# Hymba block on one core: the down projection's later groups add each product's bank straight onto the output tiles

## The chip, the core and the metric

The kernel runs on one core of a Trainium2 chip. The metric is device time in microseconds of one execution, as the median of several runs. A core has TensorE (PE in the profile; its weight loads are PEld), VectorE (DVE), ScalarE (ACT) and GpSimd (POOL), each with its own in-order queue, and SyncE (SP), whose queue issues this kernel's DMAs. TensorE writes its results to PSUM, which has eight banks of 128 x 512 float32 here; VectorE and ScalarE read them from there.

## What is computed

One decoder block on 2048 positions of width 1024, in float32: a normalised input projection, gated linear attention beside a short gated convolution, an output projection, and a SwiGLU feed-forward part. The change lies in the last product of the feed-forward part.

```python
def reference(x, norm1_g, w_in, ..., w_ffn_gate, w_ffn_up, w_ffn_down, norm_f_g):
    ...
        x = x + mixed
        h2 = rmsnorm(x, norm2_g[l])
        ffn = (jax.nn.silu(h2 @ w_ffn_gate[l]) * (h2 @ w_ffn_up[l])) @ w_ffn_down[l]
        x = x + ffn
    return rmsnorm(x, norm_f_g)
```

`w_ffn_down` is 2816 x 1024.

## The kernel before

All large products run with the positions as columns, 512 at a time, in two halves of two column blocks (j = 0, 1). Each float32 operand is split into a high and a low part (`split`, lines 152 to 154): ScalarE writes the high half (L153), VectorE the difference (L154). A product step (`product_step`) is then three matmuls: high by high, high by low, low by high (L381 to L383).

A `unit` computes a 2 x 2 block of outputs (two row tiles r, two column blocks j) with seven products in place of eight, by Strassen-Winograd combinations. `unit_weights` loads four raw quarters of the weights, lets GpSimd make four combinations (L364, L365, L366, L371), and splits seven operands into tiles `wq`, of which there are four buffers. Three PSUM banks serve a unit. Bank `oa` holds the first product and goes on being summed up through the third, fifth and seventh; bank `ob` takes the second and the sixth; the fourth has a bank of its own. In between, the banks are read: before the change, ScalarE copies (L401, in `copied`) take the first product as c11, the second as c22 and the sum of first and third as c12, into tiles of the pool `tp` or, with `into`, into tiles given by the caller. VectorE additions (L405, in `plus`) then add the fourth product to c11, bank `oa` as it stands after the fifth to c22, and bank `ob` after the sixth to c12. The fourth output, c21, is returned as the bank itself when there is no `into`. A product that goes on summing in a bank has to wait until that bank has been read.

The feed-forward part of a half is `ffn_up` (22 units over eleven column pairs m, whose results are split and stored in DRAM) and then `ffn_down`. The down projection's 2816 rows are cut into four groups of m: the first of two pairs, the three later ones of three (`GROUPS`). In each group four units run, one for each pair d0 of the eight row tiles of the output. The first group writes the output tiles y through `into`. The later groups call `unit` without it and add each result onto y (L982): c11, c22 and c12 by GpSimd, c21 by VectorE out of its bank; in the last group of the second half c12 goes to VectorE as well. In the second and third group GpSimd also adds the residual x1 onto two y tiles a unit (L989). In the last group of the first half every y is stored (`store`, L148), to be normalised later; in that of the second half ScalarE squares it (L790, L793), GpSimd sums the squares (L794), and the last four outputs are made by `last_unit`, which does not call `unit`. So 12 + 11 = 23 units belong to the later groups.

Seven of the eight y pairs of a half lie in slots of the pool `opp` (28 buffers), which also holds all operands; the next stage's operands (`load_h2`) are loaded into slots as they come free, on SP's queue behind the stores that were put ahead of them.

The code's order is not that of the engines: the framework plans the order of instructions on every engine ahead of time, from a simulated timeline (`schedule_with_timeline_sim=True`), and keeps data dependencies with semaphores. At run time each queue goes strictly in the planned order.

Of the kernel before, what the change touches and what calls it, by code (L numbers as in the profile page):

```python
# [14 lines left out]
ALU = mybir.AluOpType  # L15
# [36 lines left out]
def tile_hymba_block(ctx, tc, x, xt, win, wa, wgu, wout, wffn, wdown, wdown_first, small, out):  # L52
    nc = tc.nc
    act, dve, pool, pe = nc.scalar, nc.vector, nc.gpsimd, nc.tensor
# [80 lines left out]
    def bank(name="mm"):  # L135
        return ps.tile([P, PB], F32, name=name, tag="mm")

    def tt(name):
        return tp.tile([P, PB], F32, name=name, tag="t")

    def bt(name, shape=(P, PB)):
        return bx[0].tile(list(shape), F32, name=name, tag="b")

    def load(dst, src):
        return nc.sync.dma_start(dst, src)

    def store(dst, src):
        return nc.sync.dma_start(dst, src)  # L148
# [67 lines left out]
    def tick():  # L216
        pace[0] += 1
        if pace[0] % 2 == 0 or hurry:
            step()
        elif ahead and pace[0] % 4 == 1:  # L220
            next(ahead[0], None)
# [9 lines left out]
    def drain_background(until=lambda: False):  # L231
        while background and not until():
            step()
# [124 lines left out]
    def unit_weights(src):  # L358
        raw = raw_weights(src)
        n = src.shape[-1]  # L360
        a11, a12, a22, a21 = [raw[:, i, :] for i in range(4)]
        s1 = rawp.tile([P, PB], F32, name="s1", tag="s1", bufs=1)[:, 0:n]
        w = {"A11": weight_quarter(a11)}
        pool.tensor_tensor(s1, a21, a22, ALU.add)  # L364
        pool.tensor_tensor(a21, a11, a21, ALU.subtract)  # L365
        pool.tensor_tensor(a11, s1, a11, ALU.subtract)  # L366
        w["S1"] = weight_quarter(s1)
        w["S2"] = weight_quarter(a11)
        w["A12"] = weight_quarter(a12)
        w["S3"] = weight_quarter(a21)  # L370
        pool.tensor_tensor(a12, a12, a11, ALU.subtract)  # L371
        w["S4"] = weight_quarter(a12)
        w["A22"] = weight_quarter(a22)
        return w

    def product_step(o, w, op, k, first):
        n = len(op)
        c = slice(k * P, (k + 1) * P)
        wh, wl = w[:, 0, c], w[:, 1, c]
        xh, xl = op[k][:, 0, :], op[k][:, 1, :]  # L380
        pe.matmul(o[:], wh, xh, start=first and k == 0, stop=False, skip_group_check=True)  # L381
        pe.matmul(o[:], wh, xl, start=False, stop=False, skip_group_check=True)  # L382
        return pe.matmul(o[:], wl, xh, start=False, stop=k == n - 1, skip_group_check=True)  # L383

    def unit(src, ops, into=None):


        w = unit_weights(src)

        def mul(i, o=None):  # L390
            first = o is None
            o = bank() if first else o
            n, m = PRODUCTS[i]
            for k in range(len(ops[m])):
                product_step(o, w[n], ops[m], k, first)
            tick()
            return o

        def copied(name, o, at):
            t = tt(name) if into is None else into[at]  # L400
            act.activation(t[:], o[:], AF.Copy)  # L401
            return t

        def plus(t, o):
            dve.tensor_tensor(t[:], o[:], t[:], ALU.add)  # L405
            return t


        oa = mul(0)
        c11 = copied("c11", oa, (0, 0))  # L410
        ob = mul(1)
        c22 = copied("c22", ob, (1, 1))
        mul(2, oa)
        c12 = copied("c12", oa, (0, 1))
        plus(c11, mul(3))
        mul(4, oa)
        plus(c22, oa)
        mul(5, ob)
        plus(c12, ob)
        mul(6, oa)  # L420
        if into is not None:
            copied("c21", oa, (1, 0))
        return [(0, 0, c11, False), (1, 1, c22, False), (0, 1, c12, False), (1, 0, oa, True)]

# [101 lines left out]
    def build_h():  # L526


        def quad(k, j):
            return scaled(col(C_G1 + k), rbs[j], raws[j, k])  # L530

        return build_first(quad, first_weights)
# [255 lines left out]
    def sum_squares(ssq, y, first):  # L788
        if first:
            act.activation(ssq[:], y, AF.Square)  # L790
        else:
            q = tt("q")
            act.activation(q[:], y, AF.Square)  # L793
            pool.tensor_tensor(ssq[:], ssq[:], q[:], ALU.add)  # L794
# [138 lines left out]
    def act_op(half, m, n):  # L933
        o = opp.tile([P, 2, PB], F32R, name="op", tag="op")
        load(o[:].bitcast(F32), s_act[half][m][n][:])
        return o

    def ffn_down(half):

        y, early = {}, {}  # L940

        def group_op(m, n):
            return early.pop((m, n)) if (m, n) in early else act_op(half, m, n)

        for u, m0 in enumerate(GROUPS):
            ms = range(m0, m0 + (3 if u else 2))
            last = m0 == LAST_GROUP
            if last:
                drain_background()
            ops = {n: [group_op(m, n) for m in ms] for _, n in PRODUCTS}  # L950
            if last and half:
                begun = set()
                ssq = [
                    tiny.tile([P, PB], F32, name=f"ssx{j}", tag=f"ssx{j}", bufs=1) for j in range(2)
                ]
            for d0 in range(0, KD, 2):
                src = wdown[4 * u - 4 + d0 // 2] if u else wdown_first[d0 // 2]
                if u == 0 and d0 == 2:

                    order = [(m, n) for _, n in PRODUCTS for m in range(GROUPS[1], GROUPS[2])]  # L960
                    for m, n in order[:EARLY]:
                        early[m, n] = act_op(half, m, n)
                if u == 0:
                    for d in (d0, d0 + 1):
                        if d < KD - 1:
                            pair = opp.tile([P, 2, PB], F32, name="y", tag="op")
                        for j in range(2):
                            y[d, j] = pair[:, j, :] if d < KD - 1 else bt("y")[:]
                    unit(src, ops, {(r, j): y[d0 + r, j] for r in range(2) for j in range(2)})
                    continue  # L970
                xs = []
                if u < 3:
                    for d in (d0, d0 + 1):
                        xs.append((y[d, u - 1], bt("x1")))
                        load(xs[-1][1][:], s_x1[2 * half + u - 1][d][:])
                if last and half and d0 == KD - 2:
                    last_unit(src, ops, [act_op(half, m, "B12") for m in ms], y, ssq)
                    break
                for r, j, c, p in unit(src, ops):
                    yy = y[d0 + r, j]  # L980
                    eng = dve if p or last and half and r != j else pool
                    eng.tensor_tensor(yy, c[:], yy, ALU.add)  # L982
                    if last and half:
                        sum_squares(ssq[j], yy, j not in begun)
                        begun.add(j)
                    elif last:
                        store(s_x1[2 * half + j][d0 + r][:], yy)
                for yy, x1 in xs:
                    pool.tensor_tensor(yy, x1[:], yy, ALU.add)  # L989
        if half == 0:  # L990
            ahead[:] = [finish_later(half)]

    def finish_later(half):

        ssq = [
            tiny.tile([P, PB], F32, name=f"ssx{j}", tag=f"ssx{j}", bufs=1) for j in range(2)
        ]
        for j in range(2):
            for d in range(KD):
                y = bt("y")  # L1000
                load(y[:], s_x1[2 * half + j][d][:])
                yield
                sum_squares(ssq[j], y[:], d == 0)
        yield
        rb = [bank("rb_ps"), None]
        yield from both_rstd(ssq, rb)
        for j in range(2):
            if j:
                rb[1] = bank("rb_ps")
                act.activation(rb[1][:], ssq[1][:], AF.Copy)  # L1010
            for d in range(KD):
                y = bt("y")
                load(y[:], s_x1[2 * half + j][d][:])
                yield
                dve.scalar_tensor_tensor(y[:], y[:], col(C_GF + d), rb[j][:], ALU.mult, ALU.mult)
                store(out[2 * half + j, :, d, :], y[:])
# [59 lines left out]
    ops, first, differences = build_h()  # L1076
# [9 lines left out]
    ops = load_pairs(s_h1)  # L1086
# [122 lines left out]
```

## Time and profile before

| | us |
|---|---|
| median of 3 runs | 2098.65 |
| lowest and highest run | 2098.31, 2102.15 |
| profiled execution, its own time | 2102.39 |
| its span, first to last instruction | 2100.5 |
| TensorE busy in the span | 2034.6 |
| later groups of the first half, about | 1257 to 1435 of the span |
| later groups of the second half, about | 1900 to 2067 of the span |

Rows of groups read: line, engine, operation, output<-inputs, shapes, count | busy us, mean ns of one | idle time of the engine before them, and what ended it. Rows of waits read: who <- for whom: us in total, times, longest. Rows of a timeline read: start, duration, engine, line, operation, tiles, [idle time before <- what ended it]. A matmul's row of 0.39 us overlaps with the next; the distance of starts is what a matmul takes. DVE, ACT and POOL rows of L153 and L154 are the weight splits; tiles named c are results of a unit, y the output tiles, wq split weights, raw weights as loaded, mm a bank. Lines are those of the kernel before.

### The profile page before, as it was taken

What the parts mean: (1) busy time and instruction counts of PE and PEld (TensorE: products, weight loads), DVE (VectorE), ACT (ScalarE), POOL (GpSimd) and SP (SyncE); (2) the same over time, 40 slices, a digit from 0 to 9 for tenths busy, and PEclk for the clock granted to TensorE, in tenths of its full rate; (3) what the DMA queues carried; (4) which work ended last, traced back from release to release, by engine and by line L of the source; (5) the groups of instructions that cost most, each with busy time, mean ns of one, the idle gap of its engine ahead of it and who ended that gap; (6) DMA issues with size and microseconds to landing.
All of it is one profiled execution on the core that took longest, in us unless ns stands there. A gap on an engine that the chain in (4) does not pass through costs nothing.

```text
span 2100.5 us, 26873 instructions
## 1 busy us (share of the span) xinstructions
PE 2034.6 (97%) x9133; PEld 1649.8 (79%) x9133; DVE 1420.2 (68%) x1983; ACT 1003.2 (48%) x1990; POOL 971.9 (46%) x703
## 2 busy tenths in 40 slices
PE   6999999999999999999999999999999999999996
PEld 4768888877888878788888878787888888877774
DVE  7669786549743786788887665555767766665554
ACT  6555455656542345545545443333545444453344
POOL 3436322222102464465464338774655445436764
PEclk9999999999999999999999999999999999999998
DMA  7359495425686873655646687698444554587673
GB/s 279 129 167 318 128 340 158 149 81 167 205 281 236 325 251 105 236 200 214 223 175 220 236 314 269 234 344 321 159 178 165 192 210 174 213 340 271 259 270 110
DMA packets 189241, 464.43 MB, mean 221 GB/s; under 512 B 19824, under 2 KB 65072, under 8 KB 179504
## 3 DMA queue, kind: packets, MB, share of 16 engines
q1 hardware_dynamic: 189104, 462.72, 61.1%
q8 instruction: 72, 1.18, 0.2%
q14 instruction: 65, 0.53, 0.1%
HBM read 297.49 MB, written 165.15 MB: 220 GB/s over the span
## 4 chain that ended last, share of the span: by engine, by line
PE 74%; DVE 10%; DMA 8%; issue 3%; POOL 3%; ACT 3%; SPq 0%; DVEq 0%; POOLq 0%; ACTq 0%
PE mm L381 22%; PE mm L383 22%; PE mm L382 22%; DVE wq L154 2%; DVE h L508 2%; PE mm L812 1%; DVE op L154 1%; PE mm L813 1%; PE mm L815 1%; DVE so L154 1%; DMA raw<-in_wffn_dram 1%; DMA raw<-in_wdown_dram 1%; DMA op<-shT 1%; PE a_ps L576 1%; DVE c L405 1%
## 5 line engine op out<-in xcount | busy, mean ns | idle before, releaser
L381 PE MATMUL mm<-op,wq 128*128 128x512 f32 x2499 | 981.6, 395 | 17.8 <-ACT wq L153 7.4
L382 PE MATMUL mm<-op,wq 128*128 128x512 f32 x2499 | 976.9, 391 | 0.0
L383 PE MATMUL mm<-op,wq 128*128 128x512 f32 x2499 | 966.4, 392 | 10.4 <-DVE wq L154 9.6
L154 DVE TENSOR_TENSOR wq<-raw,wq 128x512 fp32r<-128x512 f32 (+2 forms) x626 | 527.7, 850 | 333.2 <-ACT wq L153 330.4
L153 ACT ACTIVATE wq<-raw 128x512 fp32r<-128x512 f32 (+2 forms) x626 | 363.5, 587 | 548.6 <-PE mm L383 391.5
L381 PEld LDWEIGHTS mm<-op,wq 128*128 128x128 f32 x2499 | 471.1, 189 | 132.0 <-ACT wq L153 13.5
L383 PEld LDWEIGHTS mm<-op,wq 128*128 128x128 f32 x2499 | 471.1, 189 | 121.2 <-DVE wq L154 22.6
L382 PEld LDWEIGHTS mm<-op,wq 128*128 128x128 f32 x2499 | 471.1, 189 | 97.0 <-issue 1.0
L366 POOL TENSOR_TENSOR raw<-s,raw 128x512 f32<-128x512 f32 (+2 forms) x97 | 127.6, 1316 | 422.6 <-DVE wq L154 402.5
L405 DVE TENSOR_TENSOR c<-mm,c 128x512 f32<-128x512 f32 x267 | 183.0, 685 | 94.4 <-PE mm L383 92.1
L364 POOL TENSOR_TENSOR s<-raw 128x512 f32<-128x512 f32 (+2 forms) x97 | 129.4, 1334 | 205.3 <-DMA raw<-in_wffn_dram 98.7
L371 POOL TENSOR_TENSOR raw<-raw 128x512 f32<-128x512 f32 (+2 forms) x97 | 126.8, 1307 | 129.6 <-DVE wq L154 122.4
L401 ACT ACTIVATE c<-mm 128x512 f32<-128x512 f32 x267 | 155.0, 586 | 39.0 <-PE mm L383 37.7
L794 POOL TENSOR_TENSOR ssx<-ssx,q 128x512 f32<-128x512 f32 x52 | 75.8, 1470 | 158.7 <-ACT q L793 158.5
L365 POOL TENSOR_TENSOR raw<-raw 128x512 f32<-128x512 f32 (+2 forms) x97 | 135.1, 1392 | 4.0
L982 POOL TENSOR_TENSOR y<-c,y 128x512 f32<-128x512 f32 x66 | 98.7, 1497 | 57.3 <-DVE c L405 53.2
L154 DVE TENSOR_TENSOR so<-t,so 128x512 fp32r<-128x512 f32 x100 | 90.7, 913 | 24.4 <-ACT so L153 24.0
L153 ACT ACTIVATE wq<-s 128x512 fp32r<-128x512 f32 (+2 forms) x97 | 56.8, 586 | 98.7 <-PE mm L383 86.0
L812 PE MATMUL mm<-op,wq 128*128 128x512 f32 x256 | 100.9, 395 | 0.0
L813 PE MATMUL mm<-op,wq 128*128 128x512 f32 x256 | 99.8, 390 | 0.0
L154 DVE TENSOR_TENSOR wq<-s,wq 128x512 fp32r<-128x512 f32 (+2 forms) x97 | 84.0, 866 | 17.0 <-ACT wq L153 16.4
L153 ACT ACTIVATE so<-t 128x512 fp32r<-128x512 f32 x100 | 62.5, 626 | 37.8 <-DMA sa_B<-so 16.1
(181 smaller groups left out, 1880.3 us busy)
## 6 DMA issues: line engine op xcount, KB each, us to landing
raw<-in_wffn_dram SPq DMA_DIRECT2D x44, 1024.0 KB, 6.1
sa_T<-so SPq DMA_DIRECT2D x88, 512.0 KB, 4.9
op<-sa_T SPq DMA_DIRECT2D x88, 512.0 KB, 9.4
sa_B<-so SPq DMA_DIRECT2D x69, 512.0 KB, 3.4
op<-sa_B SPq DMA_DIRECT2D x69, 512.0 KB, 9.0
raw<-in_win_dram SPq DMA_DIRECT2D x23, 1024.0 KB, 5.4
raw<-in_wdown_dram SPq DMA_DIRECT2D x24, 768.0 KB, 6.1
sx<-y SPq DMA_DIRECT2D x48, 256.0 KB, 3.3
```

What stands on the lines that cost most here:

```text
L153: last_hi[:] = [act.activation(hi, src, AF.Copy)]
L154: return dve.tensor_tensor(lo, src, hi.bitcast(F32), ALU.subtract)
L364: pool.tensor_tensor(s1, a21, a22, ALU.add)
L365: pool.tensor_tensor(a21, a11, a21, ALU.subtract)
L366: pool.tensor_tensor(a11, s1, a11, ALU.subtract)
L371: pool.tensor_tensor(a12, a12, a11, ALU.subtract)
L381: pe.matmul(o[:], wh, xh, start=first and k == 0, stop=False, skip_group_check=True)
L382: pe.matmul(o[:], wh, xl, start=False, stop=False, skip_group_check=True)
L383: return pe.matmul(o[:], wl, xh, start=False, stop=k == n - 1, skip_group_check=True)
L401: act.activation(t[:], o[:], AF.Copy)
L405: dve.tensor_tensor(t[:], o[:], t[:], ALU.add)
L812: pe.matmul(o[e, j][:], wh, m[:, 0, :], start=k == 0, stop=False)
```

## The change

`unit` gets a second way to deliver: with `onto`, a dictionary of output tiles, `copied` does not copy but adds the bank onto the tile with VectorE, and the three later `plus` calls add onto the same tiles, since `copied` returns them. With `onto`, as with `into`, the fourth result is taken out of its bank by `copied` as well. The later groups pass their y tiles as `onto`; the loop that followed keeps the sums of squares and the stores, and loses its additions. Each of the 23 units has then seven VectorE additions from PSUM onto y, and no L401 copy and no GpSimd addition of its results. Inputs, products and DMAs are the same; the order in which the summands reach y is another.

```diff
-    def unit(src, ops, into=None):
+    def unit(src, ops, into=None, onto=None):
...
         def copied(name, o, at):
+            if onto is not None:
+                return plus(onto[at], o)
             t = tt(name) if into is None else into[at]
             act.activation(t[:], o[:], AF.Copy)
             return t
...
         plus(c12, ob)
         mul(6, oa)
-        if into is not None:
+        if into or onto:
             copied("c21", oa, (1, 0))
         return [(0, 0, c11, False), (1, 1, c22, False), (0, 1, c12, False), (1, 0, oa, True)]
...
-                for r, j, c, p in unit(src, ops):
+                onto = {(r, j): y[d0 + r, j] for r in range(2) for j in range(2)}
+                for r, j, *_ in unit(src, ops, onto=onto):
                     yy = y[d0 + r, j]
-                    eng = dve if p or last and half and r != j else pool
-                    eng.tensor_tensor(yy, c[:], yy, ALU.add)
                     if last and half:
                         sum_squares(ssq[j], yy, j not in begun)
                         begun.add(j)
```

## The prediction

> **What bounds the kernel now.** I read the page's busy table first, then the busy time by stretches of the span, then the waits of TensorE, then the timeline around the longest of them.
>
> ```profile
> span 2100.5 us, 26873 instructions
> PE 2034.6 (97%) x9133; PEld 1649.8 (79%) x9133; DVE 1420.2 (68%) x1983; ACT 1003.2 (48%) x1990; POOL 971.9 (46%) x703
> ```
>
> TensorE is busy 97% of the span, and the change leaves its matmuls as they are. So the change can only move the time in which TensorE stands still or runs at a reduced clock. The stretches say where that is; columns are engine busy time, granted clock, DMA share and rate.
>
> ```profile
> core 0: us, PE busy (x) PEld busy (x) DVE busy (x) ACT busy (x) POOL busy (x), PEclk, DMA share, GB/s
> 1000.00:1195.00 195.00, 194.78 (x859) 160.86 (x858) 146.19 (x174) 97.45 (x172) 99.66 (x68) 1.00 0.54 200
> 1257.00:1435.00 178.00, 176.99 (x776) 144.74 (x775) 97.43 (x134) 62.87 (x124) 131.25 (x101) 1.00 0.79 297
> 1435.00:1480.00 45.00, 41.76 (x174) 33.18 (x173) 24.53 (x26) 17.55 (x32) 23.98 (x17) 0.96 0.56 217
> 1480.00:1880.00 400.00, 397.58 (x1744) 326.57 (x1744) 279.39 (x360) 196.42 (x354) 194.40 (x139) 1.00 0.57 207
> 1900.00:2067.00 167.00, 161.55 (x695) 130.12 (x694) 93.57 (x123) 66.55 (x130) 121.14 (x95) 0.99 0.63 237
> ```
>
> The second and fifth rows (1257 to 1435 and 1900 to 2067) hold the later groups of the two down projections, 23 units in all: the only place that the change edits. TensorE stands idle there for 178.00 - 176.99 = 1.0 us and 167.00 - 161.55 = 5.5 us. The first and fourth rows are stretches of the gate/up projection, used below as a yardstick. GpSimd is at 74% and 73% in the two edited stretches, against 51% and 49% in the yardsticks; VectorE at 55% and 56% against 75% and 70%.
>
> Who TensorE waits for in 1900 to 2067, and the longest of these waits in TensorE's timeline, with what ScalarE and GpSimd did shortly before:
>
> ```profile
> PE mm L381 <- ACT c L401: 2.9, 2, 2.6
> ...
> PE mm L381 <- ACT wq L153: 2.3, 2, 1.8
> ```
>
> ```profile
> 1924.80 1.29 POOL L982 TENSOR_TENSOR y<-c,y 128x512 f32<-128x512 f32 x1
> ...
> 1928.59 0.99 POOL L366 TENSOR_TENSOR raw<-s,raw 128x384 f32<-128x384 f32 x1
> ...
> 1929.61 1.35 ACT L153 ACTIVATE wq<-raw 128x384 fp32r<-128x384 f32 x3 [0.55 <-POOL raw L366]
> ...
> 1930.18 0.50 PE L381 MATMUL mm<-op,wq 128*128 128x512 f32 x1 [1.76 <-ACT wq L153]
> ...
> 2034.41 0.39 PE L383 MATMUL mm<-op,wq 128*128 128x512 f32 x1
> 2037.38 0.62 PE L381 MATMUL mm<-op,wq 128*128 128x512 f32 x1 [2.59 <-ACT c L401]
> ...
> 2036.21 0.63 ACT L793 ACTIVATE q<-y 128x512 f32<-128x512 f32 x1 [0.83 <-DVE y L982]
> 2036.75 1.07 ACT L401 ACTIVATE c<-mm 128x512 f32<-128x512 f32 x2
> ```
>
> The clock just after 2037, as a row of the same view by stretches:
>
> ```profile
> 2037.60:2041.00 3.40, 3.40 (x9) 2.61 (x9) 0.45 (x1) 0.83 (x2) 2.80 (x3) 0.50 0.74 231
> ```
>
> At 2037 a bank's copy (L401) stood in ScalarE's queue behind a square (L793) that itself waited for an output tile; after that wait the clock is at 0.50 for 3.40 us, which costs another 3.40 x 0.50 = 1.7 us. At 1930 split weights were late: ScalarE waited for GpSimd's combination L366, which had stood behind output additions (L982). So the loss in the edited stretches is 1.0 + 5.5 + 1.7 = 8.2 us. That is the ceiling of what the edit can give inside them.
>
> **The change, part by part.** The groups of the two stretches, first half then second half:
>
> ```profile
> L405 DVE TENSOR_TENSOR c<-mm,c 128x512 f32<-128x512 f32 x36 | 24.8, 688 | 17.0 <-PE mm L383 17.0
> ...
> L982 DVE TENSOR_TENSOR y<-mm,y 128x512 f32<-128x512 f32 x12 | 8.2, 686 | 6.1 <-PE mm L383 6.0
> ...
> L982 POOL TENSOR_TENSOR y<-c,y 128x512 f32<-128x512 f32 x36 | 55.0, 1531 | 30.4 <-DVE c L405 30.3
> ...
> L401 ACT ACTIVATE c<-mm 128x512 f32<-128x512 f32 x37 | 21.6, 583 | 12.0 <-PE mm L383 12.0
> ...
> L982 POOL TENSOR_TENSOR y<-c,y 128x512 f32<-128x512 f32 x30 | 43.7, 1457 | 26.9 <-DVE c L405 22.9 <-DMA raw<-in_wdown_dram 2.2 <-DMA x<-sx 1.8
> ...
> L982 DVE TENSOR_TENSOR y<-c,y 128x512 f32<-128x512 f32 x3 | 2.0, 679 | 0.0
> ```
>
> *Removed:* 23 x 3 = 69 ScalarE copies at 0.583 us (40 us), 66 GpSimd additions (55.0 + 43.7 = 98.7 us) and three VectorE additions in the last group. All of it lies beside TensorE's work, so only the 8.2 us can come back. *Added:* 69 VectorE additions from a bank, at the 0.688 us of L405, so 69 - 3 = 66 more VectorE instructions, 45 us net. They lie beside the products too: a unit is 7 products of 9 matmuls, and at 195.00 us for 859 matmuls (0.227 us each) a product lasts 2.04 us. VectorE's load becomes (97.4 + 36 x 0.688) / 178 = 69% and (93.6 + 30 x 0.688) / 167 = 68%, still below the 75% and 70% at which the yardstick stretches lose only 0.22 and 2.42 us of TensorE. Were that cover gone, the 66 additions would cost their 45 us.
>
> It may be less load than that. The weight splits on VectorE differ widely from one to the next:
>
> ```profile
> L154 DVE TENSOR_TENSOR wq<-raw,wq x74: 542/583/1664, 1257.2 to 1434.8; 128x384 fp32r<-128x384 f32 x68, 128x512 fp32r<-128x512 f32 x6
> ...
> L405 DVE TENSOR_TENSOR c<-mm,c x267: 659/685/693, 83.5 to 2060.7; 128x512 f32<-128x512 f32 x134
> ...
> 1259.12 1.02 POOL L365 TENSOR_TENSOR raw<-raw 128x384 f32<-128x384 f32 x1
> ...
> 1259.20 1.35 DVE L154 TENSOR_TENSOR wq<-raw,wq 128x384 fp32r<-128x384 f32 x1 [1.45 <-ACT wq L153]
> ```
>
> A split reads two SBUF tiles and takes 0.54 to 1.66 us (1.35 in the last row, beside a GpSimd addition); an addition that reads a bank takes 0.66 to 0.69 wherever it stands. The change removes 98.7 of GpSimd's 131.3 + 121.1 us, so fewer splits should meet it. I book nothing for it.
>
> *Added wait.* Three times a unit a later product reuses a bank that ScalarE's copy used to free (the third, fifth and sixth product); now VectorE's addition frees it. Behind such an addition stand, in VectorE's queue, the low halves of the next unit's weights (L154), for which TensorE waits in turn. The existing code has one such release in a unit (the seventh product behind `plus(c22, oa)`), and the waits for L405 over the whole kernel are:
>
> ```profile
>   PE mm L381: 2.2, 3
> ```
>
> That is 2.2 us over (267 + 24) / 3 = 97 units, 0.023 us each; for 69 releases 1.6 us. The bounds: 0 if the 2.04 us of the product between hides all, and 69 x (0.688 - 0.583) = 7.2 us if the longer release lay open every time. I take 1.6, the rate of the same operation in this kernel. [...]
>
> *Moved.* The y tiles of the first half's last group are final without GpSimd, so 12 of their 16 stores on SP's queue can go earlier, past the loads of the next stage's operands behind them. TensorE's waits in 1435 to 1480:
>
> ```profile
> PE mm L381 <- ACT c L401: 1.7, 1, 1.7
> PE mm L381 <- DMA op<-shT: 1.5, 1, 1.5
> ...
> 1457.40:1460.70 3.30, 3.30 (x8) 2.61 (x9) 2.57 (x4) 1.44 (x3) 1.27 (x1) 0.50 0.64 206
> ```
>
> The stretch loses 45.00 - 41.76 = 3.2 us and 3.30 x 0.50 = 1.7 us of clock: 4.9. Bounds 0 and -4.9. I take 0: most operand loads wait for slots that only TensorE's last products free, and the DMA engines are 79% busy up to 1435. No DMA is added. The ScalarE squares and GpSimd's sums of squares keep their number; what is late next where GpSimd falls away is the weight chain of ScalarE and VectorE.
>
> *The sum.* After the change I expect the edited stretches to lose what the yardsticks lose, (0.22 + 2.42) / 595 x 345 = 1.5 us, and 1.6 us for the new releases: 3.1 in place of 8.2, a gain of 5.1 us. The profiled execution took 2102.39 us (span 2100.5 and 1.9 around it), so it would take 2097.3; it is 3.7 above the median of 2098.65, and I carry the gain over to the median: **2093.6 us**.
>
> **The rivals.**
>
> *Earlier stores as well.* The transition's 4.9 us fall away too: 2088.7. For it: a wait for an operand's landing there. Against: the busy DMA engines.
>
> *The loss stays, or isn't in the median run.* The profiled execution is 3.7 us over the median; if its long stall and slow clock at 2037 make that difference, only 5.1 - 3.7 = 1.4 us remain: 2097.3. The same holds if the new instruction order, which is planned afresh, brings back weights that come late, since 2.3 us of TensorE's waits are for them.
>
> *The slow clock isn't the wait's.* The rows show TensorE idle for 2.59 us and then the clock at 0.50. If the slow stretch comes anyway, 1.7 us of the gain go: 2095.3. [...] Both slow stretches quoted follow an idle TensorE, so the trace rather speaks against that.
>
> *Slower: VectorE's queue is the bound.* If an addition that frees a bank stands behind two drawn-out splits, it ends 2 x 1.66 + 0.69 = 4.0 us after its product, 2.0 us beyond the product between, and TensorE stops for that. Without new waits the gain is 8.2 - 1.5 = 6.7 us, so 4 such events eat it, and from 6 it is slower by more than 0.2%. At one in three units, 8 x 2.0 = 16, it is 9.3 us slower: 2108. For it: VectorE takes all seven releases and is strictly in order. Against: the yardsticks, where it is busier and releases one bank a unit.
>
> **How the numbers follow.** Chances: forecast 0.38, earlier stores 0.08, loss stays 0.25, clock 0.06, slower 0.23. A measurement of this kernel can tell about 0.2%, 4.2 us. The forecast lies just beyond that at 2094.45, and I count a little of it as no change: faster 0.44, same 0.33, slower 0.23. The range goes from 2087, a little below the second case, to 2106, which takes in the slower case up to 7 events and leaves its tail out. The forecast's own range is 2091 to 2096, from releases that cost nothing to 4 us.
>
> **What would show it.** No L401 and no GpSimd row with y<-c,y between 1257 and 1435 or 1900 and 2067; about 36 and 30 more L405 there, at 0.69 us; GpSimd's share falling from 74% to about 43% (131.3 - 55.0 of 178); TensorE idle in both together under 3 us, with no clock of 0.50 around 2037. A wait of PE for L405 of more than 5 us in these stretches would show the slower case, a wait for weights of the old size the third. The prediction is wrong if the stalls move to a place that no row here shows, such as the last 34 us.

## The result, and the profile after

| | before | after |
|---|---|---|
| median of 6 runs, us | 2101.72 | 2090.53 |
| lowest and highest, us | 2098.31, 2104.18 | 2085.95, 2092.94 |
| profiled execution, its own time, us | 2102.39 | 2092.78 |
| ratio to before, 95% interval | | 0.9935 (0.9923 to 0.9947) |

By the ratio the change makes the kernel faster by 0.65%, that is 13.7 us of 2101.72, with 11.1 to 16.2 as the interval's ends; the two medians differ by 11.2. The page of the changed kernel begins:

```profile
span 2090.8 us, 26872 instructions
PE 2029.0 (97%) x9133; PEld 1648.4 (79%) x9133; DVE 1434.0 (69%) x2049; ACT 970.1 (46%) x1921; POOL 876.7 (42%) x637
```

VectorE has 66 instructions more, ScalarE 69 and GpSimd 66 fewer, as the diff says. Line numbers after the edit are larger by two in the edited part of `unit` and up to the edited loop, where L405 is now L407 and L401 is L403, and by one behind it. The kernels of the experiments have line numbers of their own. Busy time by stretches, placed by the same work as in the prediction's table (the stretch 1195 to 1257 of before, the first group of the first half, is added, as 1198.8 to 1259.3):

```profile
core 0: us, PE busy (x) PEld busy (x) DVE busy (x) ACT busy (x) POOL busy (x), PEclk, DMA share, GB/s
...
1198.80:1259.30 60.50, 58.09 (x251) 46.37 (x250) 39.99 (x64) 29.19 (x64) 21.21 (x22) 1.00 0.87 339
1259.30:1435.70 176.40, 176.10 (x775) 144.99 (x774) 105.29 (x168) 46.94 (x90) 78.17 (x65) 1.00 0.79 301
1435.70:1478.50 42.80, 40.63 (x174) 31.81 (x173) 23.70 (x26) 17.52 (x32) 23.35 (x16) 1.00 0.57 223
1478.50:1878.40 399.90, 397.48 (x1745) 326.60 (x1744) 278.69 (x360) 195.95 (x354) 195.37 (x139) 1.00 0.57 207
1898.30:2057.50 159.20, 158.48 (x696) 129.95 (x695) 100.01 (x151) 52.53 (x99) 79.34 (x65) 1.00 0.65 250
```

The two edited stretches hold 1471 matmuls in both kernels and went from 178.0 + 167.0 = 345.0 us to 176.4 + 159.2 = 335.6: 9.4 us. The transition behind the first went from 45.0 to 42.8, the first group's stretch from 62.0 to 60.5. GpSimd is busy for 44% and 50% of the edited stretches. TensorE's waits in the first and the second of them are now these alone:

```profile
PE mm L383 <- DVE wq L154: 0.3, 1, 0.3
...
PE mm L383 <- DVE wq L154: 0.6, 1, 0.6
```

None is for a bank's release. The groups of VectorE in the first edited stretch, after:

```profile
L407 DVE TENSOR_TENSOR y<-mm,y 128x512 f32<-128x512 f32 x82 | 56.5, 690 | 62.8 <-PE mm L383 62.7
L154 DVE TENSOR_TENSOR wq<-raw,wq 128x384 fp32r<-128x384 f32 x68 | 44.2, 649 | 5.7 <-ACT wq L153 5.7
```

and one row of before that the prediction did not show:

```profile
L154 DVE TENSOR_TENSOR wq<-raw,wq 128x384 fp32r<-128x384 f32 x68 | 54.1, 804 | 49.7 <-ACT wq L153 49.7
```

The same 68 weight splits take 649 ns each in place of 804, 10 us less on VectorE; in the second half's later groups the mean falls from 859 to 707. The additions from a bank stay at 0.69 us. GpSimd's additions are gone there, but that is not the whole of it: with these additions moved to VectorE and the copies left alone (`e1_adds_only` below), the first half's splits still take 734 ns:

```profile
L154 DVE TENSOR_TENSOR wq<-raw,wq 128x384 fp32r<-128x384 f32 x67 | 49.0, 734 | 34.8 <-ACT wq L153 34.6
```

VectorE's idle time now lies in front of the additions, 62.7 us of waiting for TensorE's products, and hardly in front of the splits, 5.7 us of waiting for high halves in place of 49.7. That this means weights made ahead of need is not shown by the row alone: it falls to 12.6 with the copies on VectorE too (`e2_copies_only`), where no time is gained.

Runs of most kernels here spread over 6 to 11 us, so I compare stretches of the traces, one execution each, beside the times. The table gives the time between the same two matmuls, counted in the order of their starts (the 5401st, 5621st, 6401st, 6601st, 8391st and 9061st, and the end of the span), as worked out from the starts in each trace; under "before" in us, the others as a difference from it. "After, once more" is `e0_after`; the rows below it are the runs of the next section.

```
                    first    later     transition  gate/up   later     end
                    group    groups    behind it   second    groups
                    half 1   half 1                half      half 2
before              55.4     180.0     50.7        411.3     161.8     36.8
after               -1.6      -1.5     -2.2         -0.2      -8.1      0.0
after, once more     0.0      -1.4     -1.7         +1.6      -8.6      0.0
additions only      -1.6      -1.0     +0.1         +1.8      -1.1     +0.4
copies only          0.0      +0.7     +1.6         -0.4      +0.4     -0.6
first half only     -1.6      -1.3     -0.2         -0.1      +0.8      0.0
second half only    -1.6      +0.1     +0.2         +2.2      -8.9      0.0
squares later        0.0       0.0     +0.1         -0.1      -3.6      0.0
additions, squares  -1.6      -1.3     -2.1         +2.5      -5.6     +0.5
releases later      -1.5      +2.4     -1.3         +0.2      +1.8     +0.1
additions doubled   -1.6     +53.5     -3.4         +0.1     +47.9     +1.9
end reordered       -1.6      -1.2     -2.0         +2.0      -8.7     -4.1
```

The changed kernel's row adds up to -13.6 us, but its span is only 9.7 us shorter: this execution reached the first of these matmuls 3.8 us later (1208.5 against 1204.7). No edit touches the code up to there, and the twelve executions differ in it by 7 us (1201.3 to 1208.5), so part of the spread of times has nothing to do with the edits. The columns of the later groups hang on the edit; with the transition they make 11.8 us in one execution of the changed kernel and 11.7 in the other. The first and the fourth column jump by 1.5 to 2.5 whatever the edit is. In the first column, before and the second execution of the changed kernel have a stretch of half clock there (PEclk 0.50) and the first execution of the changed kernel has not (1.00), which is taken up in the last section; that the fourth jumps for the same reason is my estimate, from the 1.7 us (3.4 x 0.50) that such a stretch costs.

### The profile page after: what moved, and what is told of

It reads as the page before. It is cut to its first block, busy times and chain, and to the rows that moved or that the text cites. A ratio compares the mean times of both kernels' runs of the same rounds, so it can differ in the third digit from the quotient of the medians.

```text
span 2090.8 us, 26872 instructions
## 1 busy us (share of the span) xinstructions
PE 2029.0 (97%) x9133; PEld 1648.4 (79%) x9133; DVE 1434.0 (69%) x2049; ACT 970.1 (46%) x1921; POOL 876.7 (42%) x637
## 4 chain that ended last, share of the span: by engine, by line
PE 77%; DVE 10%; DMA 6%; issue 3%; ACT 2%; POOL 2%; SPq 1%; DVEq 0%; ACTq 0%; POOLq 0%
PE mm L381 22%; PE mm L383 22%; PE mm L382 22%; DVE wq L154 2%; DVE h L510 2%; PE mm L814 2%; PE mm L815 2%; PE mm L817 2%; DMA op<-shT 1%; DVE so L154 1%; DVE op L154 1%; PE a_ps L578 1%; DMA shT<-so 1%; SPq L145 1%; PE o_ps L738 1%
## 5 line engine op out<-in xcount | busy, mean ns | idle before, releaser
L383 PE MATMUL mm<-op,wq 128*128 128x512 f32 x2499 | 962.4, 391 | 11.7 <-DVE wq L154 11.2
L154 DVE TENSOR_TENSOR wq<-raw,wq 128x512 fp32r<-128x512 f32 (+2 forms) x626 | 506.7, 815 | 243.2 <-ACT wq L153 241.4
L407 DVE TENSOR_TENSOR y<-mm,y 128x512 f32<-128x512 f32 x185 | 127.4, 689 | 123.3 <-PE mm L383 122.6
L407 DVE TENSOR_TENSOR c<-mm,c 128x512 f32<-128x512 f32 x198 | 135.6, 685 | 64.6 <-PE mm L383 63.3
L796 POOL TENSOR_TENSOR ssx<-ssx,q 128x512 f32<-128x512 f32 x52 | 76.2, 1479 | 160.7 <-ACT q L795 160.5
L403 ACT ACTIVATE c<-mm 128x512 f32<-128x512 f32 x198 | 114.8, 586 | 16.2 <-PE mm L383 14.8
L154 DVE TENSOR_TENSOR wq<-s,wq 128x512 fp32r<-128x512 f32 (+2 forms) x97 | 79.7, 822 | 4.1 <-ACT wq L153 3.5
```

The source lines that it names most:

```text
L154: return dve.tensor_tensor(lo, src, hi.bitcast(F32), ALU.subtract)
```

## The experiments

**One part at a time.** First, GpSimd's additions go to VectorE and ScalarE's copies stay (`e1_adds_only`, on the kernel before):

```diff
-                    eng = dve if p or last and half and r != j else pool
+                    eng = dve
```

> The kernel before with one part of the change: the additions of c11, c22 and c12 onto y go from GpSimd to VectorE (two SBUF inputs); ScalarE's copies stay. Theory 1, two separate queues: GpSimd's additions held up the weight combinations, ScalarE's copies stood behind squares. Then this part takes away the waits for late weights at 1343 (1.2 us) and 1930 (2.0) and some of the transition (up to 2.7), and leaves the wait for L401 near 2037 with its slow clock (4.5): 3 to 6 us faster than before. Theory 2, the bank release by ScalarE was all: 0 to 1 us faster. Theory 3, a new plan of the order moves stalls at random: any sign, with stalls at new places.

Measured: ratio 0.9989 (0.9978 to 1.0001), 2.3 us faster with the interval touching zero, below the 3 to 6 of theory 1, though the interval reaches 4.6; in the later groups 1.0 and 1.1 us. Second, the copies go to VectorE and GpSimd's additions stay (`e2_copies_only`):

```diff
...
         def copied(name, o, at):
             t = tt(name) if into is None else into[at]
-            act.activation(t[:], o[:], AF.Copy)
+            if later:
+                dve.tensor_copy(t[:], o[:])
+            else:
+                act.activation(t[:], o[:], AF.Copy)
...
-                for r, j, c, p in unit(src, ops):
+                for r, j, c, p in unit(src, ops, later=True):
```

> The kernel before with the other part: in the later groups the three copies of a unit go from ScalarE to VectorE, GpSimd's additions stay. Theory 1: the wait for L401 near 2037 and its slow clock fall away (4.5 us, with the one at 2053 5.1), the late weights stay: 4 to 6 us faster than before, GpSimd still at about 73% in the later groups. Theory 2: nearly the whole gain, 9 to 13 us faster. Theory 3: any sign.

Measured: ratio 0.9997 (0.9987 to 1.0007), no change; +0.7 and +0.4 us in the later groups. Neither part alone comes near 13.7 us. Theory 2 falls, and so does theory 1's sum of two separate gains, whose 4 to 6 us for the copies did not come. Theory 3 can't be ruled out for a single run, since each edit has the order planned anew; against it, the first and the fourth column of the table differ from before by less than 1 us once 1.7 us are set aside for a half clock. The waits of TensorE in the second half's later groups with the additions on VectorE, and then with the copies on VectorE, its longest waits with each:

```profile
PE mm L381 <- ACT c L401: 3.3, 2, 2.2
PE mm L383 <- DVE wq L154: 1.6, 2, 0.9
```

```profile
PE mm L381 <- DVE c L402: 3.0, 2, 2.7
PE mm L381 <- ACT wq L153: 2.8, 3, 1.7
```

The wait for late weights shrinks where GpSimd is relieved, as theory 1 said. But the wait for the bank's copy stays in both, behind ScalarE's copy in the one and behind VectorE's in the other. So the copy was not the cause; it only stood last in a chain. That chain, from the trace with the copies on VectorE, in order of time (start, duration, what; here L793 and L796 are squares, L985 the additions onto y, L408 the addition from a bank into c and L402 the copy):

```profile
2028.16 1.54 POOL y L985
...
2029.73 0.02 ACT ssx L793
...
2030.27 0.52 ACT wq L153
...
2030.81 0.56 DVE wq L154
2031.37 0.60 DVE c L408
2031.97 0.97 DVE wq L154
2032.94 0.61 DVE y L985
...
2033.57 0.64 ACT q L796
...
2034.87 0.52 ACT wq L153
...
2035.41 0.57 DVE wq L154
2035.98 0.60 DVE y L985
2036.58 0.67 DVE wq L154
2037.25 0.61 DVE c L402
...
2037.90 0.50 PE mm L381
```

It goes in a circle through in-order queues. A square on ScalarE waits for an output tile y; behind the square stand high halves of weights; VectorE's low halves wait for those; and behind a low half stands the addition that makes the next y. The two laps here, from one y to the next, last 4.8 us (2028.16 to 2032.94) and 3.0 us, and at the end TensorE stops. In the kernel before, the chain ahead of the stop at 2037 makes the same laps, from GpSimd's addition at 2027.75 over the squares at 2033.17 and 2036.21, and ends in ScalarE's copy.

**One half at a time**, on the changed kernel, with the old loop where `onto` is None (`e3_first_half`, and `e4_second_half` with `half == 1`):

```diff
+                onto = onto if half == 0 else None
...
```

> The change in the first half's down projection alone. By the two traces of before and after, TensorE gained there 1.0 us in the later groups and 2.7 in the transition behind them: 3 to 4 us faster than before if these are the change's own; within 1 us of before if they are chance, above all the slow clock at 1457.

> The change in the second half's down projection alone. By the two traces TensorE gained 7.9 us there: 7 to 9 us faster than before if the stalls at 1930 and 2037 stand in every execution; 3 to 5 if the stall at 2037 and its slow clock come only in some. With the first half alone it should add up to the whole change, about 11 to 13 us.

Measured: 0.9969 (0.9956 to 0.9981) for the first half, 0.9955 (0.9941 to 0.9968) for the second: 6.5 and 9.5 us, together 16.0, within the whole change's interval but above the 11 to 13 expected; the first half alone was expected at 3 to 4. In the traces the first half's later groups give 1.3 us and the transition 0.2, the second half's groups 8.9. The rest of the first half's 6.5 us I can't lay to the edit: its profiled execution was already 3.4 us ahead of before's when it reached the first group. In the second half alone TensorE hardly stands still at all:

```profile
1902.00:2063.00 161.00, 160.91 (x707) 132.17 (x706) 99.36 (x152) 54.88 (x101) 79.49 (x65) 1.00 0.65 248
```

**The squares behind the next weights.** To test the circle, the kernel before with the squares of a unit put behind the next unit's splits in ScalarE's queue (`e8_squares_later`); copies and additions are those of before:

```diff
...
-                for r, j, c, p in unit(src, ops):
+                us = unit(src, ops)
+                if last and half:
+                    with tc.issue_after(last_hi[0].ins):
+                        for yy, j in waiting:
+                            sum_squares(ssq[j], yy, j not in begun)
+                            begun.add(j)
+                    waiting = []
+                for r, j, c, p in us:
...
                     if last and half:
-                        sum_squares(ssq[j], yy, j not in begun)
-                        begun.add(j)
+                        waiting.append((yy, j))
```

> The kernel before with one edit: in the second half's last group the squares of a unit's outputs stand in ScalarE's queue behind the next unit's weight splits. Copies, VectorE additions and GpSimd additions are those of before. The first four runs left open what the stall at 2037 is, since it stays at 2.6 us with the additions on VectorE and at 3.1 with the copies on VectorE. Theory A: a square that waits for an output tile holds the high halves of the weights behind it, and the output tile comes late because it takes copy, addition and addition after its product. Then moving the squares takes the stall at 2037 and its slow clock away (4.5 us, and 0.5 at 2053): 3 to 6 us faster than before. Theory B: the order or the load of VectorE alone does it, the squares don't matter: within 1 us of before, the stall at 2037 stays over 2 us.

The same edit on top of the additions by VectorE (`e9_both`):

> The additions of c11, c22 and c12 onto y by VectorE in place of GpSimd, and the squares behind the next unit's splits; ScalarE's copies stay. By theory A this joins the two reliefs, late weights behind GpSimd's additions and squares at the head of ScalarE's queue, and comes near the whole change: 7 to 12 us faster than before. By theory B it is like the additions alone: 0 to 5 us faster.

Measured: 0.9996 (0.9985 to 1.0007) for the squares, so the time alone shows no gain; 0.9976 (0.9964 to 0.9987), 5.0 us, for both, below the expected 7 to 12. The traces say more. With the squares moved, TensorE's waits in the second half's later groups are

```profile
PE mm L381 <- ACT wq L153: 2.2, 2, 1.8
PE mm L383 <- DVE wq L154: 1.5, 1, 1.5
```

The waits for L401 are gone, with ScalarE's copies still in place, and so is the half clock (PEclk 1.00 there). In return five squares now stand at one spot ahead of a high half, and TensorE waits for the low half that is made from it:

```profile
2058.65 0.50 PE L383 MATMUL mm<-op,wq 128*128 128x512 f32 x1 [1.45 <-DVE wq L154]
```

The stretch gains 3.6 us in this execution. With GpSimd relieved as well it gains 5.6, near the 1.1 + 3.6 = 4.7 of the two parts, as two separate hold-ups would give. Theory A holds for the place: the square is what led to the stop at 2037 and its half clock. It does not hold for the times: the interval leaves the squares alone at most 3.2 us of the expected 3 to 6. The remaining 2.5 to 3.3 us up to the whole change's 8.1 to 8.9 take in the new wait behind the moved squares, which with both edits is the longest of

```profile
PE mm L383 <- DVE wq L154: 2.5, 3, 1.5
```

Whether the copies have a share of their own was not tried.

**The price of an addition that frees a bank.** On the changed kernel, VectorE makes one more addition of the same bank, into a tile that nobody uses, ahead of the first, second and third addition of a unit (`e5_late_release`), and then ahead of all seven (`e6_all_doubled`, the same line inside `plus`):

```diff
             if onto is not None:
+                if name != "c21":
+                    dve.tensor_tensor(tt("junk")[:], o[:], onto[at], ALU.add)
                 return plus(onto[at], o)
```

> The changed kernel with one suspected cost raised: ahead of the additions that free a bank for a later product (first, second and third product of a unit) VectorE makes one more addition of the same bank into a tile that nobody uses, 69 in all at 0.69 us. The results are the same. If the 2.04 us of the product between hide the release with room to spare, as the changed kernel's trace without a wait for these additions says: within 3 us of the changed kernel (about 2091). If VectorE's queue is close to being the bound: 69 x 0.3 to 0.7, 20 to 48 us slower than the changed kernel.

> The changed kernel with all seven additions of a unit in the later groups doubled in the same way, 161 more at 0.69 us, 111 us of VectorE. Its load in the later groups rises from 60% to over 90%, and a product's share, two additions and a split, 2 x 0.69 + 0.65 = 2.03 us, comes to the 2.04 us that a product lasts. If the price of an addition decides only from there: 5 to 30 us slower than the changed kernel. If it is hidden even then: within 3 us. If VectorE was the bound already: the whole 111 us.

Measured: 1.0007 (0.9995 to 1.0019), so these 69 additions, 48 us of VectorE, take back the whole gain; against the changed kernel's 0.9944 in its second timing that is about 13 us, between the two expectations, on average 0.19 us for each. The trace has the loss in a few places. TensorE's waits for these additions in the second half's later groups are

```profile
PE mm L381 <- DVE y L409: 6.1, 4, 3.7
```

and two of them, 3.75 us at 2039 and 1.48 us at 2057, make most of it, with a half clock behind the first (starts 0.43 us apart from 2041.25 on). In the first half such waits are 0.8 us, and the 2.4 us of the table are mainly a stop for late weights at the very end of its column.

With all doubled, 1.0487 (1.047 to 1.0504), 102 us slower than before and some 114 slower than the changed kernel. The expectations of a hidden price fail. The size is that of the third case, in which VectorE is the bound and the whole 111 us show, but VectorE is not full. The later groups of the first half with the releases late, and with all additions doubled:

```profile
1259.00:1437.00 178.00, 175.93 (x772) 144.15 (x771) 125.50 (x201) 46.84 (x89) 77.36 (x64) 1.00 0.80 299
```

```profile
1259.00:1487.00 228.00, 188.31 (x759) 150.34 (x758) 161.16 (x249) 46.08 (x87) 73.75 (x64) 0.93 0.64 237
```

VectorE is busy for 71% in both, in the second because the stretch has grown with the stops; within the changed kernel's 176.4 us the same work would be 91%, so it would still fit. With all doubled, VectorE's timeline shows the additions in bunches, here three unused ones and then three onto y, and the chain has TensorE starting again only behind the second of those:

```profile
1345.76 1.89 DVE L408 TENSOR_TENSOR junk<-mm,y 128x512 f32<-128x512 f32 x3
1347.56 0.55 DVE L154 TENSOR_TENSOR wq<-raw,wq 128x384 fp32r<-128x384 f32 x1
1348.02 1.88 DVE L409 TENSOR_TENSOR y<-mm,y 128x512 f32<-128x512 f32 x3
```

```profile
1349.36 0.50 PE mm L381
```

TensorE's waits for them in the first and the second half's later groups are

```profile
PE mm L381 <- DVE y L409: 38.5, 11, 3.6
...
PE mm L381 <- DVE y L409: 37.1, 11, 4.1
```

about one a unit, 75.6 us in all. Half clock follows these waits (PEclk 0.93 over the 228 us of the first stretch, 0.91 over 230 in the second), which costs another 16 + 21 = 37 us. Waits and half clock make up the loss. With the releases late there were two such bunches ahead of a stop. That the bunching decides, and not the higher load as such, is my reading of the traces; a higher load in another order was not tried.

**The end of the kernel.** The profile of the changed kernel, like that of before, shows six scalings of the first column block on VectorE ahead of the last product's addition (L1060). The end with one edit, the scalings behind that addition (`e7_tail`), next to the changed kernel itself in the same session (`e0_after`):

```diff
-                dve.tensor_tensor(yy, o[:], yy, ALU.add)
+                added = dve.tensor_tensor(yy, o[:], yy, ALU.add)
...
         for j in range(2):
-            scale(j, rbs[j])
+            with tc.issue_after(added.ins):
+                scale(j, rbs[j])
```

> The changed kernel with one more edit at its end: the scaling of the first column block by VectorE stands behind the last product's addition. In the profile of the changed kernel, as in that of before, six scalings (3.7 us) stand ahead of that addition while TensorE has long finished, and the end of the kernel hangs on it. Expected: 3 to 4 us faster than the changed kernel if the six scalings then fit into the waits of the last normalisation; 0 to 1 if they are only moved to the end.

> The changed kernel once more, as the reference for the others on the same chip: 11 to 16 us faster than before.

Measured: `e0_after` 0.9944 (0.9927 to 0.9962), 2090.18 us median, 11.8 us faster than before; `e7_tail` 0.9926 (0.9913 to 0.9938), 2085.88 us, and the end shorter by 4.1 us in the trace, near the expected 3 to 4. VectorE's timeline at the end of the changed kernel, then with the edit:

```profile
2071.03 3.68 DVE L1043 TENSOR_TENSOR y<-y,rb 128x512 f32<-128x512 f32 x6 [0.66 <-ACT ssx L1037]
2074.63 0.68 DVE L1060 TENSOR_TENSOR y<-mm,y 128x512 f32<-128x512 f32 x1
2078.86 0.69 DVE L201 TENSOR_SCALAR ssx<-tot 128x512 f32<-128x512 f32 x1 [3.55 <-ACT l L199]
```

```profile
2068.67 0.69 DVE L1060 TENSOR_TENSOR y<-mm,y 128x512 f32<-128x512 f32 x1 [0.30 <-PE mm L383]
2069.28 3.67 DVE L1043 TENSOR_TENSOR y<-y,rb 128x512 f32<-128x512 f32 x6
2072.86 0.68 DVE L201 TENSOR_SCALAR ssx<-tot 128x512 f32<-128x512 f32 x1
```

The scalings now lie in VectorE's former wait of 3.55 us. The intervals of the two kernels overlap by 0.0011, so it is the trace that settles the gain. By medians this version is the fastest of all.

## Why the prediction was right, and what was off

**The direction and the place were right.** The time lies inside the range, most of the gain came out of the edited stretches, TensorE's stops at 1930 and 2037 and the slow clock behind the second are gone, and no wait for a bank's release took their place, as the step on the added wait had it. The rivals in which the loss stays, the slow clock stays or the releases decide did not come.

**That the time came so near was partly luck.** The median of before rose by 3.1 us, from 2098.65 with three runs to 2101.72 with six. Taken off the 2098.65 for which the range was written, the gain would give 2087.5 by the medians and 2085.0 by the ratio, at the range's lower end of 2087 or below it.

**The gain was more than twice the forecast**, 11.1 to 16.2 us against 5.1. In size it is nearer to the first rival, earlier stores, which forecast 10.0; but that rival's place, the transition, gave only 2.2 of its 4.9. Term by term:

- *The ceiling of 8.2 us was read too low.* I took TensorE's idle time from the busy columns. A matmul's row is 0.39 us long where starts are 0.227 apart, so the first 0.16 us of every stop hides under the row before, and a stop shorter than that hides whole. By counts, the stretches needed 776 x 0.227 = 176.2 and 695 x 0.227 = 157.8 us and took 178.0 and 167.0: a loss of 11.0.
- *The rest of 3.1 us was too high.* After the change 1471 x 0.227 = 333.9 us stand in 335.6, a rest of 1.7. The 1.6 us for new releases did not come (no such wait in the trace), and the yardstick's 1.5 was about right. 11.0 - 1.7 = 9.3, the 9.4 us measured.
- *The transition, booked at 0, gave 2.2 us*, and the first group's stretch, not booked, 1.5. The second is a half clock that did not come in this execution; the table has kernels with and without it that are alike at that place. In the transition, too, 1.7 us are a half clock (PEclk 0.50 from 1457.4 to 1460.7 before, 1.00 there in the changed kernel), but there it mostly went with the wait for the operand's landing, which shrank from 1.5 us:

```profile
PE mm L381 <- ACT c L403: 1.7, 1, 1.7
PE mm L381 <- DMA op<-shT: 0.4, 1, 0.4
```

  In the five traces where that wait is 1.5 us or more (before, additions only, copies only, second half only, squares later) the half clock came each time; in the five where it is 0.4 to 1.0 us, the changed kernel's two among them, it came once, with the first half only (-0.2 in the table, -1.7 to -2.2 for the other four). So a part of the 2.2 us is the change's, as the first rival had it; what made the wait shorter was not tried.
- *The profiled execution did stand for the median.* With six runs the median of before is 2101.72, so the rival that set its stall down to that one execution falls; both profiled kernels with the old second half, before and first half only, show it.

**Two arguments were wrong though their result held.** I explained the stop at 2037 by the copy behind a square. The copies-only run shows that the copy can go and the stop stays; the square was the part that mattered, as the run with the squares moved shows, and it waits for an output tile that comes late. In the diff, y becomes final with one VectorE addition after its last product, where a second addition followed before; ScalarE's waits for y ahead of squares fell from 10.0 us in 1900 to 2067 to 2.6 in 1898 to 2058 of the changed kernel. That this is what opens the circle is my reading, and no run took it alone. And I called VectorE's added work covered because busier stretches lose nothing. The run with late releases has VectorE at 71% and 68%, below the 75% and 70% of the yardstick, and loses about 13 us. So a share below the yardstick's is no cover; the two bunches ahead of its longest stops point to the order of the queue. Of the 0.69 us by which each of the 69 releases came later, 0.19 us showed on average. The splits beside GpSimd, which I booked at nothing, fell from 804 to 649 ns; what that is worth by itself was not tried.

## What to carry to other kernels

Ask of an in-order queue which instruction at its head waits for another engine, and follow the circle: relieving one engine of it can give nothing, and the parts of a change together can give several times their sum (here 2.3 us and no change for the parts, 13.7 for the whole). A share of busy time does not say whether a release is hidden (with VectorE at 71% and 68%, below the yardstick's 75% and 70%, about 13 us showed); add a dummy instruction ahead of it and see. And take TensorE's loss from the number of matmuls and their spacing (11.0 us here), not from its idle column (8.2 with the slow clock).

## What was not expected of the hardware

In the traces of before and after, the half clock comes in pieces of 3.4 us (2037.6 to 2041.0 for one), except that the last 15.1 and 16.8 us of the span, with TensorE busy for 2.1, are at half clock as a whole. It does not come after every equal stop. In the second edited stretch it followed a stop of 2.2 to 2.7 us in four kernels (before, additions only, copies only, first half only). In the first group of the first half, where before and after have the same two stops (starts 1.2 and 1.9 us apart in place of 0.23), it came in four of the twelve executions, those at 0.0 in the table's first column (55.4 us for before). The kernel before and one execution of the changed kernel are among them, the other execution of the changed kernel is not. The clock there, before, then in the two executions of the changed kernel:

```profile
1232.10:1235.40 3.30, 3.30 (x10) 2.52 (x9) 2.00 (x4) 1.51 (x4) 2.45 (x4) 0.50 0.71 289
```

```profile
1235.00:1238.00 3.00, 2.98 (x14) 2.26 (x13) 2.26 (x4) 1.78 (x6) 2.47 (x3) 1.00 0.59 239
```

```profile
1232.60:1235.90 3.30, 3.30 (x10) 2.53 (x9) 2.03 (x4) 1.51 (x4) 2.44 (x4) 0.50 0.76 309
```

One such piece costs 3.4 x 0.50 = 1.7 us, and such pieces are a part of what single executions differ by. What decides whether one comes after a stop is not shown by these runs.
